# Row maxima spread over 64 rows by two DMAs, and a mask added on two tiles of three: an attention stage on one core

## The chip, the cores and the metric

The kernel runs on one core of one Trainium2 chip, in one launch. Its time is the device time of that core in microseconds; the time before is the median of three runs.

## The reference

A trunk of four residual layers on 1024 tokens of width 1024: attention, an MLP, a spatial gating layer, a second MLP, and a final norm. All of the change lies in the attention layer, which has 16 query heads of width 64 in two groups of eight:

```
# group A: band of 3 blocks of 128 keys, a sink logit for each head
s = einsum('bnqhgd,bnjhd->bnhgqj', qb, kband) * scale
s = where(mask, s, -1e30)                       # |key - query| <= 128
m = maximum(max(s, axis=-1), sink_b)
p = exp(s - m);  denom = sum(p) + exp(sink_b - m)
# group B: all 1024 keys
s = einsum('bqhd,bkhd->bhqk', qblk, kf) * scale
p = softmax(s)
```

Both groups need, for each query, the largest score m before the exponentials are taken.

## The kernel before

Everything runs as float32 split into a high part and a rest, so most products are made of several 128x512 matmuls. The attention layer first projects (tiles `lin`), writes rotated q and k to DRAM (`qs_...`), and then goes through the 16 heads in the order b b a a b a b a b a b a b a b a (`heads`, line 535); I call them h0 to h15. `load_head` (line 557) brings a head's q back by three DMAs: lines 568 and 569 fill both halves of `r1` with the high part, line 570 fills rows 0 to 63 of `r2` with the rest. Where a key group is new, `load_k` (line 547) first loads `k1` and `k2` by three more.

A head has two passes. The **maxima pass** (`mx_units`, line 574) multiplies 128 queries with the keys (`mx`, queries as rows of the result), and VectorE takes the maximum of each row: line 603 for a b head, line 587 for an a head. After four query tiles the four columns of maxima are put together in a 128x4 tile `m4` (lines 606 and 593); that is one set, two sets for each head. The **score pass** (`st_units`, line 698) makes the scores transposed (`st`, keys as rows), so that a maximum has to be subtracted from a column. It is therefore put into the product: rows 64 to 127 of `r2` hold -m/64 on every row, rows 64 to 127 of `k2` hold ones, and the sum over 64 rows gives -m. ScalarE takes the exponential, and `av` multiplies with the values.

What brings `m4` to these 64 rows is `bcast` (line 611): two steps of a chain after the set is done, four matmuls of 128 columns with a -1/64 identity turn and spread it in a PSUM bank (`bc`), and VectorE copies 64 rows of that into `r2` (line 617). For an a head the band's mask is a third matmul on each `st` tile, `identn` times `maskk`, 384 columns wide (256 at the two ends of the sequence).

The heads overlap: while head n is in its score pass, the maxima pass of heads n+1 and n+2 runs in between (`mx_to`, line 763). `load_to(n + 3)` (line 755) issues the loads. The program's order on each engine is set by a scheduler when the kernel is built, and every engine then works its list strictly in turn; so does SP, which issues all DMAs, and a DMA on SP that waits holds up those listed behind it. Eight PSUM banks are shared by all of these tiles.

Of the kernel before, what the change touches and what calls it, by code (L numbers as in the profile page):

```python
# [7 lines left out]
F32 = mybir.dt.float32  # L8
F32R = mybir.dt.float32r
AF = mybir.ActivationFunctionType  # L10
# [3 lines left out]
P = 128  # L14
# [3 lines left out]
HN = 512  # L18
# [14 lines left out]
def tile_kernel(ctx: ExitStack, tc: tile.TileContext, I, out, upto=99, dbg=None):  # L33
    nc = tc.nc
    pe, act, dve, pool, sp = nc.tensor, nc.scalar, nc.vector, nc.gpsimd, nc.sync
# [7 lines left out]
    drp = ctx.enter_context(tc.tile_pool(name="drp", bufs=1, space=bass.MemoryType.DRAM))  # L43
# [3 lines left out]
    def nm(s):  # L47
        uid[0] += 1
        return f"{s}_{uid[0]}"

    def blk(s, dt=F32R):
        return blkp.tile([P, 2, HN], dt, tag="blk", name=nm(s))

    def tr(s, dt=F32):
        return trp.tile([P, HN], dt, tag="tr", name=nm(s))
# [7 lines left out]
    def ps(s):  # L63
        return psp.tile([P, HN], F32, tag="ps", name=nm(s))

    def f(ap):
        return ap.bitcast(F32)
# [3 lines left out]
    def mm(o, l, r, start, stop, **kw):  # L71
        last_mm[0] = pe.matmul(o, l, r, start=start, stop=stop, **kw)  # L72
# [226 lines left out]
    def split(dst, src, lo=None):  # L299
        act.copy(dst[:, 0], src)  # L300
        (lo or dve).tensor_tensor(dst[:, 1], src, f(dst[:, 0]), op=ALU.subtract)
# [86 lines left out]
    with tc.issue_after(w_dma[5].ins):  # L388
# [3 lines left out]
        identn = cp.tile([P, P], F32R, name="identn")  # L392
# [115 lines left out]
    maskk = cp.tile([P, 3 * P], F32R, name="maskk")  # L508
# [30 lines left out]
    R1, R2 = {}, {}  # L539
# [3 lines left out]
    def kv_of(hd):  # L543
        return (0 if hd[0] == "a" else 2) + hd[1] // 4

    def load_k(kv):
        a = blk("k1")
        b = blk("k2")
        hi, lo = (qs["k"][part, kv].rearrange("r n t -> (r n) t") for part in range(2))
        sp.dma_start(f(a[0:64].rearrange("p a b -> p (a b)")), hi)  # L550
        sp.dma_start(f(a[64:128].rearrange("p a b -> p (a b)")), lo)
        sp.dma_start(f(b[0:64].rearrange("p a b -> p (a b)")), hi)
        pool.memset(f(b[64:128]), 1.0)
        k1[kv] = a.rearrange("p a b -> p (a b)")
        k2[kv] = b.rearrange("p a b -> p (a b)")

    def load_head(n):
        hd = heads[n]
        kv = kv_of(hd)
        if kv not in k1:  # L560
            load_k(kv)
        key = f"{hd[0]}{hd[1] // 4}"
        assert all((q, half) in ready for q in (key, "k") for half in range(2))
        hi, lo = (qs[key][part, hd[1] % 4].rearrange("r n t -> (r n) t") for part in range(2))
        a, b = blk("r1"), blk("r2")
        a = a.rearrange("p a b -> p (a b)")
        b = b.rearrange("p a b -> p (a b)")
        sp.dma_start(f(a[0:64]), hi)
        sp.dma_start(f(a[64:128]), hi)
        sp.dma_start(f(b[0:64]), lo)  # L570
        R1[n], R2[n] = a, b


    def mx_units(n):
# [34 lines left out]
        return [lambda tb=tb, kh=kh: unit(tb, kh) for tb in range(8) for kh in range(2)]  # L609

    def bcast(n, half, m4):
        for _ in range(2):
            yield 1
        p_ = ps("bc")
        for i in range(4):
            mm(p_[:, i * P : (i + 1) * P], m4[:, i : i + 1].to_broadcast([P, P]), identn, i == 0, i == 3)
        dve.tensor_copy(R2[n][64:128, half * HN : (half + 1) * HN], p_[64:128])
        shifted.add((n, half))

    OLO = pool  # L620
# [14 lines left out]
    def exps_b(p_):  # L635
        e = tr("pe")
        act.activation(e, p_, AF.Exp, scale=0.125)
        pp = blk("pp")
        cnt[0] += 1
        if cnt[0] % 4:  # L640
            act.copy(pp[:, 0], e)  # L641
        else:
            dve.tensor_copy(pp[:, 0], e)  # L643
        lo = dve if cnt[0] % 8 == 2 or (cnt[0] < 10 and cnt[0] % 2) else pool
        lo.tensor_tensor(pp[:, 1], e, f(pp[:, 0]), op=ALU.subtract)  # L645
        return pp
# [3 lines left out]
    def av(n, half, kt, pp, c0, o0, w_, first, last):  # L650

        kv = kv_of(heads[n])
        if (n, half) not in AV:
            AV[n, half] = ps("av")
        o = AV[n, half][:, o0 : o0 + w_]
        if kv < 2:
            mm(o, v1[kv][:, kt, :], pp[:, c0 : c0 + w_], first, last)
        else:
            a, b = v1[kv][:, kt, :], v2[kv][:, kt, :]
            mm(o, a, pp[:, 0, c0 : c0 + w_], first, False)  # L660
            mm(o, b, pp[:, 0, c0 : c0 + w_], False, False)
            mm(o, a, pp[:, 1, c0 : c0 + w_], False, last)
        if last:
            chains.append(finish_head(n, half))

    def finish_head(n, half):
        hd = heads[n]
        o = AV.pop((n, half))
        pair, r0 = (4 if hd[0] == "a" else 0) + hd[1] // 2, 64 * (hd[1] % 2)
        if pair not in O:  # L670
            O[pair] = blk("o", F32), blk("den", F32)
        yield 1
        rs = slice(r0, r0 + 64)
        out_, den = O[pair][0][:, half], O[pair][1][:, half]
        act.copy(out_[rs], o[0:64])
        if hd[0] == "a":
            es = tr("es")
            act.activation(es[64:128], f(R2[n][64:128, half * HN : (half + 1) * HN]), AF.Exp, scale=8.0,
                           bias=par[64:128, C_SINK + hd[1] : C_SINK + hd[1] + 1])
            dve.tensor_tensor(den[rs], o[64:128], es[64:128], op=ALU.add)  # L680
        else:
            act.copy(den[rs], o[64:128])
        if hd[1] % 2 == 0:
            return
        yield 1
        y = tr("rec")
        act.activation(y, den, AF.Ln)
        act.activation(y, y, AF.Exp, scale=-1.0)
        yield 1
        dve.tensor_tensor(den, den, y, op=ALU.mult)  # L690
        dve.scalar_tensor_tensor(y, den, 2.0, y, op0=ALU.subtract, op1=ALU.mult)  # L691
        dve.scalar_tensor_tensor(out_, out_, -1.0, y, op0=ALU.mult, op1=ALU.mult)
        yield 1
        t = blk("oh")
        split(t, out_, OLO)
        OH[pair, half] = t

    def st_units(n):
        hd = heads[n]

        def need(*halves):
            assert all((n, q) in shifted for q in halves), "row maxima come too late"

        kv = kv_of(hd)
        if hd[0] == "b":
            def unit(half, kt):
                need(half)
                p_ = ps("st")
                ks, hs = slice(kt * P, (kt + 1) * P), slice(half * HN, (half + 1) * HN)
                mm(p_, k1[kv][:, ks], R1[n][:, hs], True, False)  # L710
                mm(p_, k2[kv][:, ks], R2[n][:, hs], False, True)
                pp = exps_b(p_)
                return [lambda: av(n, half, kt, pp, 0, 0, HN, kt == 0, kt == 7)]

            return [lambda half=half, kt=kt: unit(half, kt) for half in range(2) for kt in range(8)]
        keep = {}

        plan = [(0, 0, True, False), (0, 3, False, False), (0, 1, False, False), (0, 2, False, False),
                (0, 4, False, True),
                (1, 4, True, False), (1, 7, False, False), (1, 5, False, False), (1, 6, False, False),  # L720
                (1, 3, False, True)]

        def score(kb):
            lo, hi = max(kb - 1, 0), min(kb + 2, 8)
            w_ = (hi - lo) * P
            off = (lo - kb + 1) * P
            need(lo // 4, (hi - 1) // 4)
            p_ = ps("st")[:, 0:w_]
            ks = slice(kb * P, (kb + 1) * P)
            mm(p_, k1[kv][:, ks], R1[n][:, lo * P : hi * P], True, False)  # L730
            mm(p_, identn, maskk[:, off : off + w_], False, False)
            mm(p_, k2[kv][:, ks], R2[n][:, lo * P : hi * P], False, True)
            keep[kb] = (exps_a(p_, w_), lo, hi)

        def part(half, kb, first, last):
            pp, lo, hi = keep[kb]
            a, b = max(lo, 4 * half), min(hi, 4 * half + 4)
            av(n, half, kb, pp, (a - lo) * P, (a - 4 * half) * P, (b - a) * P, first, last)

        def unit(items):  # L740
            for half, kb, first, last in items:
                if kb not in keep:
                    score(kb)
            return [lambda it=it: part(*it) for it in items]

        cuts = [plan[0:1], plan[1:2], plan[2:3], plan[3:4], plan[4:6], plan[6:7], plan[7:8], plan[8:10]]
        return [lambda c=c: unit(c) for c in cuts]
# [7 lines left out]
    def load_to(n):  # L755
        while loaded[0] < min(n, 16):
            load_head(loaded[0])
            loaded[0] += 1
# [603 lines left out]
```

## Time and profile before

| | before |
|---|---|
| median of 3 runs | 2074.59 us (2074.17 to 2076.68) |
| profiled execution, its own time | 2075.91 us |
| its span | 2074.1 us |
| busy, share of the span: TensorE / VectorE / ScalarE / GpSimd | 98% / 70% / 46% / 27% |
| attention's score pass | from about 164 to 451 us |

The span is what lies between the first and the last instruction. Matmuls overlap in their pipeline, so a matmul's own duration is longer than the step from its start to the next one's start, and a high busy share does not say that TensorE goes at full pace. Waits are given with the engine's instruction and with what ended the wait.

### The profile page before, as it was taken

The numbers are of one execution on the slowest core, as the hardware profiler recorded it, in microseconds if no ns is written. First come the engines' busy times: TensorE is split into PE (matmuls) and PEld (weight loads), VectorE is DVE, ScalarE is ACT, GpSimd is POOL, SyncE is SP. The second block draws the span as 40 slices with busy tenths as digits, with TensorE's granted clock in tenths as the row PEclk, the third lists the DMA queues.
The fourth block names the chain that finished last, engine by engine and source line by source line (L and its number), as shares of the span: only waits on it lengthen the run. The fifth ranks groups of instructions, "written<-read, shape, count | busy, mean of one in ns | idle before, by whom it ended". The sixth has DMA issues, their size and how long they took to land.

```text
span 2074.1 us, 27073 instructions
## 1 busy us (share of the span) xinstructions
PE 2028.4 (98%) x9126; PEld 1672.3 (81%) x9126; DVE 1456.5 (70%) x2324; ACT 962.2 (46%) x1768; POOL 563.8 (27%) x437
## 2 busy tenths in 40 slices
PE   8998999999999999999999999999999999999997
PEld 7786877788878888888888888888788888888885
DVE  6878878855896676756696445556976767846975
ACT  5525767763533333435444434533533333544542
POOL 4324565642232222200002125422232223000021
PEclk9999999999999999999999999999999999999998
DMA  4364121134135444767364210342254446865542
GB/s 163 128 185 135 40 68 36 42 112 152 52 132 171 149 157 163 266 206 289 128 220 142 92 59 11 122 138 97 76 180 150 148 162 205 296 222 191 170 139 92
DMA packets 207307, 294.92 MB, mean 142 GB/s; under 512 B 19648, under 2 KB 88768, under 8 KB 207168
## 3 DMA queue, kind: packets, MB, share of 16 engines
q1 hardware_dynamic: 207168, 293.19, 42.7%
q8 instruction: 72, 1.18, 0.2%
q14 instruction: 67, 0.55, 0.1%
HBM read 207.13 MB, written 85.98 MB: 141 GB/s over the span
## 4 chain that ended last, share of the span: by engine, by line
PE 85%; DVE 9%; issue 2%; ACT 2%; POOL 1%; DMA 1%; SPq 0%; DVEq 0%; POOLq 0%; ACTq 0%
PE up L72 26%; PE lin L72 17%; PE dy L72 17%; PE dx L72 13%; PE av L72 4%; PE st L72 3%; PE mx L72 1%; PE vp L72 1%; DVE w L147 1%; PE kp L72 1%; DVE mb L603 1%; DVE rec L691 1%; PE bc L72 1%; DVE pp L643 1%; PE hss L72 1%
## 5 line engine op out<-in xcount | busy, mean ns | idle before, releaser
L72 PE MATMUL up<-h,w 128*128 128x512 f32 x1536 | 363.1, 389 | 5.4 <-ACT w L146 3.0
L72 PE MATMUL dy<-w,w 128*128 128x512 f32 x1536 | 364.7, 389 | 0.0
L72 PEld LDWEIGHTS up<-h,w 128*128 128x128 f32 x1536 | 288.1, 188 | 66.1 <-ACT w L146 3.4
L72 PEld LDWEIGHTS dy<-w,w 128*128 128x128 f32 x1536 | 288.3, 188 | 60.3 <-issue 0.5
L314 POOL TENSOR_TENSOR ss<-ss,sq 128x512 f32<-128x512 f32 x66 | 103.1, 1563 | 661.7 <-ACT sq L313 566.8
L72 PE MATMUL dx<-w,w 128*128 128x512 f32 x1152 | 276.7, 389 | 0.0
L72 PE MATMUL up<-w,w 128*128 128x512 f32 x1152 | 276.6, 390 | 0.0
L72 PEld LDWEIGHTS up<-w,w 128*128 128x128 f32 x1152 | 216.2, 188 | 45.8 <-ACT h L835 0.5
L72 PEld LDWEIGHTS dx<-w,w 128*128 128x128 f32 x1152 | 216.2, 188 | 44.9
L146 ACT CAST w<-wr 128x512 fp32r<-128x512 f32 x288 | 167.5, 621 | 144.7 <-DVE wr L179 39.0
L147 DVE TENSOR_TENSOR w<-wr,w 128x512 fp32r<-128x512 f32 x288 | 201.6, 709 | 23.9 <-ACT w L146 19.9
L72 PE MATMUL lin<-h,w 128*128 128x512 f32 x768 | 181.3, 393 | 1.1 <-POOL w L123 0.5
L72 PEld LDWEIGHTS lin<-h,w 128*128 128x128 f32 x768 | 143.3, 188 | 33.6 <-issue 2.4
L956 POOL TENSOR_TENSOR t<-ua,ub 128x512 f32<-128x512 f32 x32 | 44.6, 1394 | 453.0 <-ACT ua L903 423.0
L645 POOL TENSOR_TENSOR pp<-pe,pp 128x512 fp32r<-128x512 f32 x107 | 143.0, 1358 | 77.7 <-ACT pp L641 54.2
L147 DVE TENSOR_TENSOR w<-ur,w 128x512 fp32r<-128x512 f32 x224 | 155.9, 706 | 6.6 <-ACT w L146 6.4
L146 ACT CAST w<-ur 128x512 fp32r<-128x512 f32 x224 | 135.9, 620 | 43.1 <-DVE w L147 20.5
L147 DVE TENSOR_TENSOR w<-ws,w 128x512 fp32r<-128x512 f32 x128 | 93.9, 734 | 68.6 <-ACT w L146 68.1
L72 PE MATMUL st<-r,k 128*128 128x512 f32 (+2 forms) x384 | 132.1, 402 | 4.6 <-DVE mb L603 3.6
L146 ACT CAST w<-ws 128x512 fp32r<-128x512 f32 x128 | 79.5, 621 | 112.0 <-DVE ws L226 75.8
L903 ACT ACTIVATE ua<-ua 128x512 f32<-128x512 f32 x64 | 40.5, 633 | 172.7 <-DVE ua L902 172.7
L72 PE MATMUL av<-pp,v 128*128 128x512 f32 x384 | 109.2, 395 | 3.5 <-DVE pp L643 1.6
(191 smaller groups left out, 3042.5 us busy)
## 6 DMA issues: line engine op xcount, KB each, us to landing
ur<-ucd SPq DMA_DIRECT2D x224, 256.0 KB, 3.6
wr<-in_w SPq DMA_DIRECT2D x256, 128.0 KB, 2.7
ucd<-t SPq DMA_DIRECT2D x128, 256.0 KB, 2.0
wr<-in_w SPq DMA_DIRECT2D x128, 256.0 KB, 3.7
ucd<-ub SPq DMA_DIRECT2D x64, 256.0 KB, 2.0
x<-in_xT SPq DMA_DIRECT2D x32, 256.0 KB, 3.5
xmd<-x SPq DMA_DIRECT2D x32, 256.0 KB, 2.1
ucd<-ua SPq DMA_DIRECT2D x32, 256.0 KB, 2.0
```

Of the source, the lines that this page charges most:

```text
L72: last_mm[0] = pe.matmul(o, l, r, start=start, stop=stop, **kw)
L146: act.copy(w[:, 0], src)
L147: dve.tensor_tensor(w[:, 1], src, f(w[:, 0]), op=ALU.subtract)
L314: pool.tensor_tensor(sumsq[half][:, 0:w_], sumsq[half][:, 0:w_], t, op=ALU.add)
L603: dve.tensor_reduce(M[n][:, tb, kh : kh + 1], p_, axis=AX.X, op=ALU.max)
L643: dve.tensor_copy(pp[:, 0], e)
L645: lo.tensor_tensor(pp[:, 1], e, f(pp[:, 0]), op=ALU.subtract)
L691: dve.scalar_tensor_tensor(y, den, 2.0, y, op0=ALU.subtract, op1=ALU.mult)
L903: act.activation(dst, dst, AF.Square)
L956: pool.tensor_tensor(t3, ua[:, 1], ub[:, 1], op=ALU.subtract)
```

## The change

Three edits. `bcast` now waits one step of its chain instead of two and issues two DMAs on SP: one writes the 128x4 set to a row of a DRAM tile `md`, element by element (512 runs of 4 bytes), the other reads that row of 2 KB into each of 64 rows of `r2`. The matmuls `bc` and the copy at line 617 go away. The scale -1/64 moves from `r2` to `k2`'s constant rows, and the sink's exponential takes a scale of -0.125 in place of 8. And the mask's matmul covers the two outer tiles of a band alone (2x128 columns in place of 384, 128 in place of 256).

```diff
-        pool.memset(f(b[64:128]), 1.0)
+        pool.memset(f(b[64:128]), -1.0 / 64.0)
...
+    md = drp.tile([16, 2, HN], F32, tag="md", name="md")
...
     def bcast(n, half, m4):
-        for _ in range(2):
-            yield 1
-        p_ = ps("bc")
-        for i in range(4):
-            mm(p_[:, i * P : (i + 1) * P], m4[:, i : i + 1].to_broadcast([P, P]), identn, i == 0, i == 3)
-        dve.tensor_copy(R2[n][64:128, half * HN : (half + 1) * HN], p_[64:128])
+        yield 1
+
+        row = md[n, half]
+        sp.dma_start(row.rearrange("(a q) -> q a", a=4), f(m4))
+        sp.dma_start(f(R2[n][64:128, half * HN : (half + 1) * HN]), row.partition_broadcast(64))
         shifted.add((n, half))
...
-            act.activation(es[64:128], f(R2[n][64:128, half * HN : (half + 1) * HN]), AF.Exp, scale=8.0,
+            act.activation(es[64:128], f(R2[n][64:128, half * HN : (half + 1) * HN]), AF.Exp, scale=-0.125,
...
-            mm(p_, identn, maskk[:, off : off + w_], False, False)
+            if 0 < kb < 7:
+                o_, m_ = (t.rearrange("p (a b) -> p a b", a=3)[:, ::2] for t in (p_, maskk))
+            elif kb:
+                o_, m_ = p_[:, 0:P], maskk[:, 0:P]
+            else:
+                o_, m_ = p_[:, P : 2 * P], maskk[:, 2 * P : 3 * P]
+            mm(o_, identn, m_, False, False)
```

On TensorE little else moves. Around the first set of h10, at the end of h8's score pass, before (tiles of the name `st` are scores, `av` values, `mx` maxima):

```order
L72 MATMUL st_823_3354<-r1_623_2705,k1_621_2699 128x512
L72 MATMUL st_823_3354<-r2_624_2706,k2_622_2700 128x512
L72 MATMUL av_822_3348<-pp_797_3268,v1_5_93 128x512
L72 MATMUL av_822_3348<-pp_797_3268,v2_6_95 128x512
L72 MATMUL av_822_3348<-pp_797_3268,v1_5_93 128x512
L72 MATMUL bc_826_3365<-identn_204,m4_815_3330 128x128 x4
L72 MATMUL st_829_3376<-r1_706_2966,k1_704_2960 128x256
L72 MATMUL st_829_3376<-maskk_766,identn_204 128x256
L72 MATMUL st_829_3376<-r2_707_2967,k2_705_2961 128x256
```

and the same place after:

```order
L72 MATMUL st_803_3277<-r1_609_2650,k1_607_2644 128x512
L72 MATMUL st_803_3277<-r2_610_2651,k2_608_2645 128x512
L72 MATMUL av_802_3269<-pp_777_3189,v1_5_93 128x512
L72 MATMUL av_802_3269<-pp_777_3189,v2_6_95 128x512
L72 MATMUL av_802_3269<-pp_777_3189,v1_5_93 128x512
L72 MATMUL st_808_3293<-r1_689_2899,k1_687_2893 128x256
L72 MATMUL st_808_3293<-maskk_766,identn_204 128x128
L72 MATMUL st_808_3293<-r2_690_2900,k2_688_2894 128x256
```

The four `bc` matmuls are gone and the mask is half as wide; nothing else changed its place.

On SP, before, the loads of h2 (`k1_334`, `k2_335`, `r1_336`, `r2_337`) follow straight behind the last writes of q:

```order
L461 DMA qs_a1_210<-qh_277_1577 128x2x512
L461 DMA qs_a1_210<-qh_278_1581 128x2x512
L550 DMA k1_334_1762<-qs_k_208 64x1024
L551 DMA k1_334_1762<-qs_k_208 64x1024
L552 DMA k2_335_1763<-qs_k_208 64x1024
L568 DMA r1_336_1768<-qs_a0_209 64x1024
L569 DMA r1_336_1768<-qs_a0_209 64x1024
L570 DMA r2_337_1769<-qs_a0_209 64x1024
```

After, both sets of h1 (`m4_284`, `m4_326`) stand in the same list ahead of them and between them:

```order
L461 DMA qs_a1_210<-qh_276_1574 128x2x512
L617 DMA md_1148<-m4_284_1597 128x4x1
L618 DMA r2_226_1349<-md_1148 64x512
L617 DMA md_1148<-m4_326_1732 128x4x1
L550 DMA k1_331_1753<-qs_k_208 64x1024
L618 DMA r2_226_1349<-md_1148 64x512
L551 DMA k1_331_1753<-qs_k_208 64x1024
L552 DMA k2_332_1754<-qs_k_208 64x1024
L568 DMA r1_333_1759<-qs_a0_209 64x1024
L569 DMA r1_333_1759<-qs_a0_209 64x1024
L570 DMA r2_334_1760<-qs_a0_209 64x1024
```

The first load now stands behind the write of `m4_326`, the others behind the read of it.

Later on SP, before, the loads of h11 (`r1_827`) and h12 (`r1_861`) stand alone:

```order
L568 DMA r1_827_3371<-qs_a1_210 64x1024
L569 DMA r1_827_3371<-qs_a1_210 64x1024
L570 DMA r2_828_3372<-qs_a1_210 64x1024
L568 DMA r1_861_3491<-qs_b1_212 64x1024
L569 DMA r1_861_3491<-qs_b1_212 64x1024
L570 DMA r2_862_3492<-qs_b1_212 64x1024
```

After, each stands behind a set of h10 (`m4_795` its first, `m4_823` its second, both into `r2_725`):

```order
L617 DMA md_1148<-m4_795_3251 128x4x1
L618 DMA r2_725_3025<-md_1148 64x512
L568 DMA r1_806_3288<-qs_a1_210 64x1024
L569 DMA r1_806_3288<-qs_a1_210 64x1024
L570 DMA r2_807_3289<-qs_a1_210 64x1024
L617 DMA md_1148<-m4_823_3354 128x4x1
L568 DMA r1_839_3404<-qs_b1_212 64x1024
L618 DMA r2_725_3025<-md_1148 64x512
L569 DMA r1_839_3404<-qs_b1_212 64x1024
L570 DMA r2_840_3405<-qs_b1_212 64x1024
```

The loads of a head have moved behind the write and the read of a set of the head before it.

## Rows read from the trace of the kernel before

**Rows 1.** Stretches (us): busy time and count by engine, clock, DMA share, GB/s.

```profile
164.00:451.00 287.00, 270.57 (x1271) 221.58 (x1272) 233.17 (x419) 210.98 (x390) 167.89 (x127) 0.99 0.25 64
```

**Rows 2.** TensorE's waits from 186 to 430 us: waiting instruction, releaser, sum, times, longest.

```profile
PE bc L72 <- DVE m L606: 4.1, 3, 1.4
PE st L72 <- DVE mb L603: 3.0, 4, 0.9
PE bc L72 <- DVE m L593: 2.4, 3, 1.1
```

**Rows 3.** Timeline, TensorE, 299 to 302 us: start, us, engine, line, operation, count.

```profile
299.27 0.56 PE L72 MATMUL bc<-identn,m 128*128 128x128 f32 x4
299.66 0.33 PE L72 MATMUL st<-r,k 128*128 128x256 f32 x1
299.83 0.28 PE L72 MATMUL st<-maskk,identn 128*128 128x256 f32 x1
299.95 0.28 PE L72 MATMUL st<-r,k 128*128 128x256 f32 x1
...
301.38 0.34 PE L72 MATMUL st<-maskk,identn 128*128 128x384 f32 x1
301.56 0.35 PE L72 MATMUL st<-r,k 128*128 128x384 f32 x1
```

**Rows 4.** Groups by form: VectorE's copy at line 617, busy us, mean ns, idle before.

```profile
L617 DVE CAST r<-bc 64x512 fp32r<-64x512 f32 x32 | 22.2, 695 | 3.9 <-PE bc L72 2.9
```

**Rows 5.** DMA page: queue (packets, MB, share), issues (KB, us to landing).

```profile
q1 hardware_dynamic: 207168, 293.19, 42.7%
...
wr<-in_w SPq DMA_DIRECT2D x256, 128.0 KB, 2.7
...
st<-in_w_sT SPq DMA_DIRECT2D x8, 64.0 KB, 2.4
...
par<-in_par SPq DMA_DIRECT2D x1, 34.0 KB, 1.8
```

**Rows 6.** The 16 DMAs of line 569, 130 to 460 us.

```profile
DMA to landing us min/median/max: 3.9/4.7/8.0
```

**Rows 7.** Timeline, 182 to 198 us: SP, VectorE and TensorE around h2.

```profile
182.88 0.60 SPq L569 DMA_DIRECT2D r<-qs_a  x1
...
191.90 0.16 DVE L606 TENSOR_REDUCE m<-mb 128x4 fp32r<-128x8 f32 x1
...
197.84 0.28 PE L72 MATMUL mx<-k,r 128*128 128x256 f32 x1
```

**Rows 8.** Timeline, 214 to 221 us: h3's first set, h4's first maxima.

```profile
214.79 1.13 DVE L593 CAST m<-ma 128x4 fp32r<-128x4 f32 x1
...
220.83 0.39 PE L72 MATMUL mx<-k,r 128*128 128x512 f32 x1
```

**Rows 9.** Timeline, 308 to 319 us: h8's second set, h10's first maxima.

```profile
308.81 0.16 DVE L606 TENSOR_REDUCE m<-mb 128x4 fp32r<-128x8 f32 x1
...
318.38 0.39 PE L72 MATMUL mx<-k,r 128*128 128x512 f32 x1
```

**Rows 10.** Timeline, 334 to 348 us: h10's first set, h11's first maxima.

```profile
334.94 0.50 PE L72 MATMUL mx<-k,r 128*128 128x512 f32 x1
...
338.42 0.16 DVE L606 TENSOR_REDUCE m<-mb 128x4 fp32r<-128x8 f32 x1
...
347.09 0.46 PE L72 MATMUL mx<-k,r 128*128 128x256 f32 x2
```

**Rows 11.** Timeline, 439 to 450 us: the last set, weights and exponentials behind it.

```profile
439.30 0.74 DVE L593 CAST m<-ma 128x4 fp32r<-128x4 f32 x1
...
444.81 1.13 ACT L121 CAST w<-st 128x512 fp32r<-128x512 f32 x2
445.84 0.76 ACT L632 ACTIVATE ea<-st 128x256 f32<-128x256 f32 x2
...
449.85 0.59 PE L72 MATMUL av<-ea,v 128*128 128x256 f32 x2
```

## The prediction

> **What bounds the kernel now.** I began with the stretches. The change lies in the score pass of the attention layer, 287 us in which TensorE is busy for 270.6 and VectorE for 233 [rows 1]. So what counts is TensorE's list: its steps, and where it stands still. The steps I read from the timeline as start to next start, since a matmul's own duration overlaps the next: the four narrow matmuls of a set take 0.39 us together, a mask of 384 columns takes 0.18 and one of 256 columns 0.12 [rows 3]. The waits of TensorE come next: from 186 to 430 us it stood 4.1 and 2.4 us before the narrow matmuls because VectorE had the set not ready, and 3.0 us before score tiles because a PSUM bank was not yet reduced, 9.5 us in all [rows 2]. Last I looked at what stands around each set in time, since the new DMAs stand in SP's list with the loads of later heads.
>
> **What goes.** There are 32 sets (16 heads, two each). The narrow matmuls: 32 x 0.39 = 12.5 us off TensorE's list [rows 3]. They have no cover, because TensorE is the engine that sets this stage. The masks: of the eight tiles of a head six go from 384 to 256 columns, 48 x 0.06 = 2.9 us, and two from 256 to 128, where a step of 0.39 / 4 = 0.10 us in place of 0.12 gives 16 x 0.02 = 0.3 us. No row shows a matmul that reads and writes two pieces of 128 columns. It may cost what one of 256 columns does, 0.12, or two of 128, 0.20, which would turn 2.9 into a loss of 1.0; I take the first, which is nearest in columns, so 3.1 us with rounding. The waits for a set before a narrow matmul, 6.5 us, go with the matmuls. The 3.0 us before score tiles I count as gone too: VectorE loses 32 copies of 0.695 us, 22.2 us of its 233 [rows 1, 4]. That is 12.5 + 3.1 + 9.5 = 25.1 us. The constants and the sink's scale change no instruction's size: nothing. The shorter chain (one step, not two) only issues the DMAs sooner.
>
> The Trainium skill (TensorE: Matmul & The Clock Gate, Back-to-back issue gap) gives about 81 ns for a matmul of 128 columns in a stream with its weight loads. The trace has 98 ns here, and the trace decides; by the page the narrow matmuls would be worth 10.4 us in place of 12.5, and the forecast would be 2 us later.
>
> **What comes.** Each set is now a write (512 runs of 4 bytes) and, on SP, a wait until it has landed, then the read of 2 KB into 64 rows. TensorE needs the read late: a set is used tens of microseconds after it is made, so the read itself is hidden. But SP works its list in turn, and the order now has the loads of the next heads behind the write and the read of a set. Today the load of h2's `r1` is out at 182.88, 15 us before its first matmul at 197.84 [rows 7]; behind a set that lead is gone. So for each head I compare the time from the set to the first maxima matmul of the loaded head with the chain: landing of the write (W), 0.6 us for each issue on SP that stands between [rows 7], and 4.7 us from the issue of the second `r1` load to its landing [rows 6].
>
> W is in no row. Below: 34 KB in 128 runs land in 1.8 us. Above: all packets of the queue took 42.7% of 16 x 2074 us for 207168, 68 ns each; 32 for an engine add 2.2 us to 1.8, so 4.0. In between: 64 KB in 128 runs of 512 bytes land in 2.4 us, 128 KB in 256 such runs in 2.7, 0.3 us for 128 runs more, which for 512 runs makes 3.3 [rows 5]. I take 3.0 us, between the middle of the bounds and that last figure.
>
> - h2: its set is ready at 192.06, the first maxima matmul comes at 197.84, 5.8 us later [rows 7]. Behind the landing stand the read, `k1`, `k2` and the first `r1`: 3.0 + 4 x 0.6 + 4.7 = 10.1. Late by 4.3 us.
> - h4: from 215.92 to 220.83, 4.9 us [rows 8]; one narrow group less (0.4), seven value matmuls that now stand ahead (0.24 each by the steps of [rows 3], 1.7): 6.2. The chain is 3.0 + 0.6 + 4.7 = 8.3. Late by 2.1.
> - h6, h10, h12, h14: from 308.97 to 318.38, 9.4 us [rows 9], less two narrow groups and five masks: 8.3. The chain is 8.3. Just in time.
> - h8: the same with three issues more (1.8). Late by 1.8.
> - h7, h11, h13, h15: from the last maxima matmul of the set at 334.94 to the use at 347.09 are 12.15 us; without the wait of 1.4 that ended there [rows 2], a narrow group and five masks, 10.05. VectorE had the set 3.64 us after the matmul [rows 10]; two copies fewer ahead of it make 2.25, so 7.8 are left. The chain is 3.0 + 2 x 0.6 + 4.7 = 8.9. Late by 1.1, four times: 4.4.
> - h9: the same with three key loads ahead. Late by 2.9.
> - After the last set stand two weight tiles. It is ready at 440.04; the write, the read and a load bring the first tile at 448.3. ScalarE wants it for a cast at 444.81 and, working in turn, holds the exponentials behind it, which today are done at 446.6 and needed at 449.85 [rows 11]. About 4.3 us later on ScalarE, with 0.7 us of TensorE's work gone, is 1.8 us late.
>
> The sum of what is late is 4.3 + 2.1 + 1.8 + 4.4 + 2.9 + 1.8 = 17.3 us. The net is 25.1 - 17.3 = 7.8 us: the profiled execution of 2075.9 us becomes 2068.1, and as the median stands 1.3 us under that execution, 2067 is my forecast.
>
> With W = 1.8 only 6.9 us are late: 2056. With W = 4.0 the four heads that are just in time join, 13 chains in all, 13 us more: 2080.
>
> **The rivals.** *A long write makes it slower.* The place is SP's wait for a write of 4-byte runs, and the price is 13 us for each microsecond of W beyond 3.0. The gain is used up at W = 3.6, and it is slower by over 0.2% from W = 3.9. For it: no row has runs under 272 bytes, and every set is such a write. Against it: 512 runs are few, 32 for each DMA engine. At W = 4.2 the time is 2082. The Trainium skill (DMA: Bandwidth & Descriptors, Specifications) says that runs below 512 bytes are read, modified and written by the DMA engine. By that rule, with the per-run share of the upper bound doubled, W would be an estimated 6.2 us and the time about 2108.
>
> *The loads have slack that I overlook*, so that nothing is late and the whole 25.1 us are gained: 2049.5. For it: today the loads run 15 us ahead [rows 7], and a late load may fall where TensorE would have waited for VectorE. Against it: the order has them behind the sets, word for word.
>
> *VectorE's waits come back.* TensorE no longer stops before the narrow matmuls, but a little later before a PSUM bank that VectorE has not reduced; only 15.6 us are gained, 17.3 lost: 2076, no change. For it: part of today's waits are of that kind already (3.0 us, [rows 2]). Against it: VectorE has 22 us less to do, and each late load gives it time.
>
> **Chances.** Forecast, W from 1.8 to 3.4: 0.45. Long write: 0.27. Waits come back: 0.17. Slack: 0.11. About 0.2%, 4.1 us, is what a measurement of this kernel can tell from no change, so faster means under 2070.4 and slower over 2078.7. Faster: 0.43 of the forecast and 0.11 of slack, 0.54. No change: 0.02, the 0.17, and 0.04 of the long write near its turning point, 0.23. Slower: 0.23. The range of 2052 to 2083 leaves out about 0.09 on each side. The forecast's own range is 2056 to 2072.
>
> **What would show it.** In the profile after, TensorE should have no wait for a set, and waits for `r` and `k` tiles loaded from DRAM in their place: the longest at h2's first maxima matmul, about 4 us, smaller ones at h4, h8 and the a heads. The write's time to landing is W itself. A mask's step should be 0.12 us. VectorE's busy time should be 22 us less. ScalarE should wait about 4 us at the weight cast after the last set. The prediction is wrong if TensorE waits for no load at all, if W is far from 3 us, or if TensorE's waits for VectorE stay near 9 us.

## The result, and the profile after

The change makes the kernel slower: a median of 2176.86 us (2169.16 to 2181.07, six runs) against 2075.69 us for the kernel before (six runs), a ratio of 1.0482 with a 95% interval of 1.0469 to 1.0495. That is 101 us more; 2067 was forecast. The profiled execution has a span of 2167.4 us, 93.3 more than before. Nearly all of that arises in the score pass: the first matmul of the output projection comes at 544.03 us in place of 451.05, 93.0 us later.

The stretch, from 164 us to near its end (the columns are those of [rows 1]):

```profile
164.00:542.00 378.00, 277.43 (x1136) 223.08 (x1137) 213.84 (x386) 208.88 (x389) 168.58 (x127) 0.86 0.27 60
```

TensorE is busy for 277 us, a little longer than before although its list is shorter, and that in 378 us in place of 287, at a mean granted clock of 0.86 in place of 0.99. So the stage now has gaps, and a lower clock. What ended the gaps, in TensorE's waits from 160 to 543 us (against [rows 2]):

```profile
PE mx L72 <- DMA r<-qs_a: 44.8, 6, 8.6
PE st L72 <- DMA r<-md: 33.6, 8, 9.9
PE mx L72 <- DMA r<-qs_b: 15.2, 5, 5.6
PE av L72 <- POOL pp L646: 5.3, 5, 1.5
PE mx L72 <- DVE mb L605: 1.6, 2, 1.1
PE mx L72 <- DVE ma L589: 0.8, 1, 0.8
```

They sum to 101.3 us; the same view of before, from 160 to 451 us, has 16.0. The waits for VectorE are nearly gone. In their place stand 60.0 us for loaded q tiles, as foreseen in kind, and 33.6 us for the set's own read, which was thought hidden.

The issues of DMAs (KB, median us from issue to landing; against [rows 5, 6]):

```profile
r<-qs_a SPq DMA_DIRECT2D x24, 256.0 KB, 6.6
r<-md SPq DMA_DIRECT2D x32, 128.0 KB, 4.2
md<-m SPq DMA_DIRECT2D x32, 2.0 KB, 9.6
```

A write of 2 KB takes 9.6 us to land, longer than a load of 256 KB. What SP does with that is plain around h2 (timeline of SP, then of TensorE; against [rows 7]):

```profile
180.58 0.36 SPq L617 DMA_DIRECT2D md<-m  x1
189.74 0.45 SPq L618 DMA_DIRECT2D r<-md  x1
190.36 0.46 SPq L617 DMA_DIRECT2D md<-m  x1
...
199.22 0.45 SPq L618 DMA_DIRECT2D r<-md  x1
...
201.62 0.60 SPq L569 DMA_DIRECT2D r<-qs_a  x1
...
208.36 0.55 PE L72 MATMUL mx<-k,r 128*128 128x256 f32 x1 [8.60 <-DMA r<-qs_a]
```

SP issues a write, stands 9 us, issues the read, then does the same for the next set. h2's second `r1` load is issued at 201.62; it was at 182.88 before. Its first maxima matmul waits 8.60 us. Over 150 to 560 us SP's waits say the same:

```profile
SPq L618 <- DMA md<-m: 248.2, 31, 11.6
```

The write's packets don't account for its length. Between the landing of other transfers and the read of 223.90 only the write issued at 215.55 is under way. The DMA view of 216 to 223.8 us, with the busy tenths of the 16 engines in 40 slices of 0.2 us:

```profile
DMA  0057000000000090000000000000000000000000
...
DMA packets 529, 0.01 MB, mean 1 GB/s; under 512 B 528, under 2 KB 528, under 8 KB 528
```

Its 512 packets are in slices 3 and 4, so they are through 1.2 us after the issue. Then the engines do nothing for it (the lone 9 is one packet of an instruction queue) for another 7 us until the write counts as landed.

The lower clock shows behind such a gap. TensorE at 412 us:

```profile
412.10 0.87 PE L72 MATMUL mx<-k,r 128*128 128x256 f32 x2 [7.30 <-DMA r<-qs_a]
...
413.62 0.52 PE L72 MATMUL st<-r,k 128*128 128x384 f32 x1
413.94 0.41 PE L72 MATMUL st<-maskk,identn 128*128 128x256 f32 x1
414.15 0.52 PE L72 MATMUL st<-r,k 128*128 128x384 f32 x1
```

After 7.30 us without work a product of 384 columns takes 0.32 us from start to start, against 0.18 in [rows 3]: the granted clock is 0.50 from 412 to 416 us and was 1.00 in the rows before, the 1.2 GHz level in place of 2.4. At 539 us, at the higher level (1.00 from 539.2 to 540 us), the mask's two pieces of 128 columns take a step of 0.13, about what one piece of 256 columns takes in [rows 3]:

```profile
539.23 0.28 PE L72 MATMUL st<-maskk,identn 128*128 128x256 f32 x1
539.36 0.33 PE L72 MATMUL st<-r,k 128*128 128x384 f32 x1
```

### The profile page after: what moved, and what is told of

Read it like the earlier page. It is cut to its first block, busy times and chain, and to the rows that moved or that the text cites. A ratio compares the mean times of both kernels' runs of the same rounds, so it can differ in the third digit from the quotient of the medians.

```text
span 2167.4 us, 26922 instructions
## 1 busy us (share of the span) xinstructions
PE 2036.6 (94%) x8998; PEld 1674.6 (77%) x8998; DVE 1437.9 (66%) x2292; ACT 961.2 (44%) x1768; POOL 564.9 (26%) x437
## 4 chain that ended last, share of the span: by engine, by line
PE 70%; DVE 6%; DMA 3%; issue 1%; ACT 1%; POOL 1%; SPq 0%; DVEq 0%; ACTq 0%; POOLq 0%
PE up L72 25%; PE dy L72 16%; PE lin L72 14%; PE dx L72 12%; DMA md<-m 2%; PE av L72 1%; DVE w L147 1%; PE st L72 1%; DMA r<-qs_a 1%; PE mx L72 0%; PE mix L72 0%; DVE mb L605 0%; DVE d L862 0%; PE ssb L72 0%; POOL vh L301 0%
## 5 line engine op out<-in xcount | busy, mean ns | idle before, releaser
L72 PE MATMUL st<-r,k 128*128 128x512 f32 (+2 forms) x384 | 144.6, 439 | 33.7 <-DMA r<-md 33.6
L72 PE MATMUL mx<-k,r 128*128 128x512 f32 (+2 forms) x192 | 73.9, 415 | 62.5 <-DMA r<-qs_a 44.8
L72 PEld LDWEIGHTS st<-r,k 128*128 128x128 f32 x384 | 80.4, 211 | 54.5 <-DMA r<-md 30.3
```

## The experiments

My theory after the result: the write of packed 4-byte runs is long, and by SP's list it makes loads and sets late. Rivals: the mask has a part; the number of runs, or their size, makes the write long whatever their place; the short runs hold the DMA engines, so that loads are late in any list; SP's standing still as such, not the chain's length, is what is paid.

**The mask alone** (kernel before, with the last block of the diff). 

> The kernel before with the mask's edit alone; the sets still go by four matmuls and a copy. My theory (everything lost comes from the sets' DMAs, the mask's edit is worth what the prediction said): 48 x 0.06 + 16 x 0.02 = 3 us faster, a ratio of 0.9985. Rival (a matmul in two pieces of 128 columns costs two matmuls of 128): 1 us slower, a ratio of 1.0005.

Measured: 2075.01 us against 2076.68, a ratio of 0.9993 (0.9984 to 1.0002). That can't be told from no change, nor, by its upper end of 3.3 us, from the 3 us expected. Two matmuls' price, 1.0005, is outside.

**The sets alone** (the change without that block). 

> The change with its sets by DMA alone; the mask stays three tiles wide. My theory: within 5 us of the whole change, some 104 us slower than before, since the matmuls that the mask saves lie in a stage that now waits for DMAs. Rival (the mask has a part in the loss): under 90 us slower.

Measured: 2178.01 us, ratio 1.0491 (1.0477 to 1.0505). The sets' DMAs alone make a loss that can't be told from the whole one.

**128 runs of 16 bytes.**

```diff
-        sp.dma_start(row.rearrange("(a q) -> q a", a=4), f(m4))
+        sp.dma_start(row.rearrange("(q a) -> q a", a=4), f(m4))
```

> The change, but each set is written in 128 runs of 16 bytes in place of 512 runs of 4 bytes, to the same 2 KB. The maxima thus land in another order and belong to other queries, and the exponentials take a scale of 0.01 so that they stay finite. My theory (the number of runs makes the write long, and the loads wait behind it on SP): the write lands in 2.5 to 4 us in place of 9.6, TensorE's waits for r tiles fall from 94 us to under 25, and the time is 2065 to 2090. Rival (a short run's writing or DRAM's answer is long whatever their number): 8 to 10 us to land, and the time stays at 2165 to 2180.

Measured: 2072.51 us, ratio 0.9980 (0.9971 to 0.9989). The write lands in 2.2 us; TensorE waits 8.2 us for r tiles (from 160 to 450 us):

```profile
PE av L72 <- POOL pp L646: 7.0, 8, 1.5
PE mx L72 <- DMA r<-qs_a: 4.2, 1, 4.2
...
PE st L72 <- DMA r<-md: 2.1, 1, 2.1
PE mx L72 <- DMA r<-qs_b: 1.9, 2, 1.1
```

So nearly all of the loss goes with the write's form. The one load that waits long is h2's, 4.2 us.

**256 runs of 8 bytes** (as above, with `"(a q b) -> q a b", a=2, b=2`). 

> As the kernel with 16-byte runs, with 256 runs of 8 bytes for a set (the maxima again belong to other queries, exponentials with a scale of 0.01). Theory (a price for each run: 128 runs 2.2 us, 512 runs 9.6 us, so 0.019 us a run): 4.7 us to landing, and by the prediction's 13 us for each microsecond beyond W = 2.2 some 30 us over the 2072.5 of 16-byte runs: 2100. Rival (it is the size of a run: below a bound every write is long): 8 us or more, and 2150 or more; or 2 to 3 us and 2075.

Measured: 2083.81 us, ratio 1.0037 (1.0023 to 1.0051); 3.8 us to landing. The landing is a little under the count's 4.7, and the time well under the 2100 that went with it. Count and place both remain possible.

**Both DMAs of a set issued by GpSimd** (`pool.dma_start` in place of `sp.dma_start` in `bcast`). 

> The change, but the write and the read of a set are issued by GpSimd in place of SP, so that no load stands behind them; the write is as long as in the change. My theory (what counts is SP's list): the waits for r tiles loaded from q go from 60 us to under 10; GpSimd stands 9 us on each read, 45 us of its rest subtractions come late, and the time is 2080 to 2120. Rival (the short runs keep the DMA engines themselves busy, and loads are late in whatever list they stand): 2150 or more, with the loads still at 6 to 7 us to landing. Second rival (the sets themselves come too late for the scores): the waits for the set's own tile stay above 30 us.

Measured: 2250.93 us, ratio 1.0840 (1.0826 to 1.0855). TensorE's waits from 150 to 640 us:

```profile
PE st L72 <- DMA r<-md: 76.2, 9, 17.1
PE av L72 <- POOL pp L646: 75.9, 18, 10.2
```

TensorE waits for no load any more. But in the same stretch GpSimd now stands 197 us before reads of sets (27 times), and both what it subtracts and the sets themselves are late, as the second rival had it. The time expected was far off: the standing did not go, it moved to an engine that has work to do. This run does not settle whether the loads were late through the list or through the engines, since TensorE was late for other reasons.

**The read three steps later.**

```diff
         sp.dma_start(row.rearrange("(a q) -> q a", a=4), f(m4))
+        for _ in range(3 if n > 1 else 0):
+            yield 1
         sp.dma_start(f(R2[n][64:128, half * HN : (half + 1) * HN]), row.partition_broadcast(64))
```

> The change, but from the third head on the read of a set is issued three steps of its chain after the write, so that in SP's order the loads of the next head stand ahead of the read nearly everywhere; the write is as long as in the change. My theory (SP's list, not the write itself, makes the loads late): TensorE's waits for r tiles loaded from q go from 60 us to under 25, with what is left where a load stands behind an earlier read; the time is 2095 to 2140. Rival (loads are late since the short runs hold the DMA engines): the loads keep 6 to 7 us to landing, their waits stay above 45, and the time is 2160 or more.

Measured: 2168.07 us, ratio 1.0441 (1.0427 to 1.0455), 0.4% under the change. My expectation failed. The b heads' loads moved ahead of a read and their waits fell from 15.2 to 6.3 us, but those of the a heads rose from 44.8 to 53.2, behind another read. And a load that is now issued in the middle of a write lands late: the median of `r<-qs_b` from 150 to 560 us is 11.7 us, 6.0 in the change.

**The loads issued by GpSimd, the sets left on SP** (`pool.dma_start` in `load_k` and `load_head`). 

> The change, with the loads of the heads' q and k issued by GpSimd in place of SP; the sets stay on SP as in the change. If the loads are late because they stand behind the sets in SP's list: TensorE's 60 us of waits for r tiles loaded from q go to under 15, the 34 us for the set's own tile stay or grow to 50, GpSimd's list is some 50 us longer in this stage, and the time is 2105 to 2140. If they are late because a write under way holds whatever the DMA engines are given: the waits stay above 40 us and the time is 2150 or more.

Measured: 2178.99 us, ratio 1.0494 (1.0476 to 1.0511). TensorE's waits from 150 to 570 us:

```profile
PE st L72 <- DMA r<-md: 75.7, 15, 10.9
PE mx L72 <- DMA r<-qs_a: 32.3, 5, 8.3
```

Neither theory fits. The waits for loads halve, so SP's list had a part; but the waits for the sets more than double (the write now lands in 10.4 us), and the sum is 108 us where the change has 93.6. What the loads no longer wait, TensorE waits for the sets.

**One write and one read for a head** (`m8` of 128x8 after the last tile, one `bcast` for both halves). 

> The change with one write of 1024 packed runs of 4 bytes and one read of 4 KB in 64 rows for a head, in place of two sets: 16 waits of SP in place of 32. Theory (the time is SP's standing, some 8 us for each write, and packed writes wait only within a block, so twice the blocks take no longer): 8 to 11 us to landing, SP stands 130 to 160 us on reads in place of 248, and the loss of 101 us falls to about half: 2110 to 2140. Rival (each run has its price): 17 to 20 us to landing, SP stands as long as in the change, and 2165 or more. Second rival (what counts is how late a set is, not SP's standing): a set that is finished with its head comes later still, TensorE's waits for it grow beyond 34 us, and 2165 or more.

Measured: 2183.21 us, ratio 1.0517 (1.0502 to 1.0533). The write of 1024 runs lands in 9.3 us, so each run does not have its price. SP stands 142.6 us before reads in place of 248.2, as expected, and nothing is gained (SP's waits from 150 to 570 us, then TensorE's):

```profile
SPq L618 <- DMA md<-m: 142.6, 16, 10.3
SPq L617 <- DVE m L608: 94.4, 8, 15.1
SPq L617 <- DVE m L595: 82.3, 7, 20.9
```

```profile
PE st L72 <- DMA r<-md: 77.0, 11, 8.3
PE av L72 <- POOL pp L647: 16.3, 14, 2.2
...
PE mx L72 <- DMA r<-qs_a: 4.0, 1, 4.0
```

The second rival's signs came: the waits for loads are nearly gone, and those for sets are 77 us. But SP's standing as a whole did not fall: before the writes it now stands 177 us for VectorE's maxima, against 54 in the change. So this run does not show that the standing costs nothing. My reading, which no run tests alone: in all of these variants the chain of a write of 9 us and a read is longer than the lead that the order gives a set or a load; only where TensorE meets it changes.

**Eight forms of the write, beside the kernel before** (an extra write and a read of one element behind each set). 

> The kernel before, with a second write of each set to DRAM in one of eight forms, four sets each, and behind it on SP a read of one element of what was written, whose issue shows when the write has landed; nothing uses what is read. Forms: 512 runs of 4 bytes packed in 2 KB (as in the change), the same 64 bytes apart, the same 512 bytes apart; 128 runs of 4 bytes packed in 512 bytes, the same 512 bytes apart; 128 runs of 16 bytes packed in 2 KB, the same 512 bytes apart; 256 runs of 8 bytes packed in 2 KB. Theory of the count (each run has its price): 512 runs take 8 to 10 us however far apart, 128 runs of 4 bytes 2 to 3 us, 256 runs 4 us. Theory of the place (writes into one block of DRAM wait for each other; a block of 512 bytes takes 128, 64 or 32 runs in the three packed forms, which landed in 9.6, 3.8 and 2.2 us): 512 runs 512 bytes apart land in 2 to 4 us, and 128 packed runs of 4 bytes in 8 to 10 us.

Measured: 2104.06 us (one run). SP's waits before the reads of one element, summed over up to four sets of a form (150 to 520 us):

```profile
SPq L581 <- DMA fd<-m: 33.7, 4, 9.5
SPq L590 <- DMA fd<-m: 30.5, 4, 8.6
...
SPq L602 <- DMA fd<-m: 13.8, 4, 3.9
...
SPq L587 <- DMA fd<-m: 4.5, 3, 1.7
...
SPq L596 <- DMA fd<-m: 3.3, 4, 1.1
```

Each line is one form, five of the eight. From the issue of the write to that of the read behind it, by SP's timeline, without the one pair in which two writes overlapped:

```
line  form                                     us, write to read       runs in 64 bytes
581   512 runs of 4 bytes, packed              8.3, 8.9, 9.0, 10.0     16
590   128 runs of 4 bytes, packed              7.1, 7.9, 8.2           16
602   256 runs of 8 bytes, packed              3.3, 3.9, 4.1, 4.3       8
596   128 runs of 16 bytes, packed             1.4 four times           4
584   512 runs of 4 bytes, 64 bytes apart      2.2, 2.2, 3.6, 6.1       1
587   512 runs of 4 bytes, 512 bytes apart     1.8, 1.9, 2.1, 2.3       1
593   128 runs of 4 bytes, 512 bytes apart     1.4, 1.4, 1.4, 2.5       1
599   128 runs of 16 bytes, 512 bytes apart    1.4, 3.0, 3.0            1
```

The place decides. A quarter of the packed 4-byte runs takes nearly as long as all of them; the same 512 runs 512 bytes apart take a fifth. (The 6.1 was issued among loads.) The time grows with the number of runs that share a small stretch of memory, and 64 bytes apart is nearly far enough (2.2 to 3.6 us, against 1.8 to 2.3 at 512 bytes). With the two columns, an estimate is some 0.5 us for each run in such a stretch (8 us for 16, 4 for 8), as if each waited for the one before; for 4 it would give 2 us, and 1.4 was measured, no more than for runs that lie apart. Why it is so is not shown, and in the packed forms a run's size and the number of runs in 64 bytes change together, so the forms show that the place decides, not the law. The Trainium skill (DMA: Bandwidth & Descriptors, Specifications) has every transfer below 512 bytes read, modified and written. It gives no price, and here the size alone does not make a write long: runs of 4 and of 16 bytes land quickly too when they lie apart (1.4 to 3.0 us at 512 bytes).

**The change with its 512 runs 64 bytes apart.**

```diff
-    md = drp.tile([16, 2, HN], F32, tag="md", name="md")
+    md = drp.tile([16, 2, HN * 16], F32, tag="md", name="md")
...
-        sp.dma_start(row.rearrange("(a q) -> q a", a=4), f(m4))
-        sp.dma_start(f(R2[n][64:128, half * HN : (half + 1) * HN]), row.partition_broadcast(64))
+        sp.dma_start(row.rearrange("(a q s) -> q a s", a=4, s=16)[:, :, 0], f(m4))
+        sp.dma_start(f(R2[n][64:128, half * HN : (half + 1) * HN]), row[0:HN].partition_broadcast(64))
```

> The change with the same 512 runs of 4 bytes for a set, but 64 bytes apart in DRAM (32 KB for a set, filled with zeros once beforehand); the read takes the first 2 KB of that as 64 rows of 2 KB, so the maxima aren't subtracted, and the exponentials take a scale of 0.01. Number and size of the runs, both DMAs of a set and SP's order are those of the change. Theory of the place (packed 4-byte writes wait for each other in DRAM): 2 to 3.6 us to landing and 2070 to 2085, like 128 packed runs of 16 bytes. Theory of the count or of the size of runs: 8 us or more and 2160 or more.

Measured: 2068.54 us, ratio 0.9965 (0.9953 to 0.9978), 2.0 us to landing. With the same runs, the same two DMAs and the same order on SP, the loss is gone (what else differs is a fill with zeros beforehand and the exponentials' scale). TensorE's waits from 160 to 570 us, those for DMAs first of all:

```profile
PE av L72 <- POOL pp L650: 8.9, 9, 1.5
PE mx L72 <- DMA r<-qs_a: 3.8, 1, 3.8
...
PE st L72 <- DMA r<-md: 1.3, 1, 1.3
...
PE mx L72 <- DMA r<-qs_b: 0.3, 1, 0.3
```

**No transport at all.** 

> The change without any transport of the sets: no write, no read, no narrow matmul, no copy; the 64 rows are filled by one more load of q's rest for a head (256 KB, 16 in all), and the exponentials take a scale of 0.01, so that the result is not the reference's. It shows the most that the edits could gain. The prediction's sum: 25.1 us, so 2050. Theory that waits come back (TensorE meets VectorE, GpSimd and ScalarE a little later): 12.5 + 3.1 us and at most 3 of the 9.5 us of waits, so 2057 to 2061.

Measured: 2062.42 us against 2076.15, ratio 0.9930 (0.9916 to 0.9943): by the medians 13.7 us is about the most that the edits could gain (the spans of the profiled executions, 2074.1 and 2058.5 us, differ by 15.6). TensorE's waits from 160 to 447 us:

```profile
PE av L72 <- POOL pp L643: 7.3, 9, 1.4
PE mx L72 <- DVE mb L605: 4.6, 5, 1.5
PE st L72 <- DVE mb L605: 2.0, 4, 1.1
PE av L72 <- DVE mb L605: 1.5, 1, 1.5
PE st L72 <- DVE w L428: 1.5, 2, 0.8
PE mx L72 <- ACT ea L630: 0.7, 1, 0.7
PE st L72 <- DVE den L678: 0.5, 2, 0.2
```

They sum to 18.1 us. The waits for sets are gone, and more than as much stands before other tiles.

**A set turned before it is written.** One matmul turns 128x4 into 4x128, and each run has 512 bytes; the kernel before otherwise, with the mask's edit.

```diff
+        mm(p_[0:4, 0:P], m4, identn, True, True)
+        t4 = t4p.tile([4, P], F32, tag="t4", name=nm("t4"))
+        dve.tensor_copy(t4, p_[0:4, 0:P])
+        sp.dma_start(row.rearrange("(a q) -> a q", a=4), t4)
+        sp.dma_start(f(R2[n][64:128, half * HN : (half + 1) * HN]), row.partition_broadcast(64))
```

> The kernel before with the mask's edit, and a set turned by one matmul of 4 rows x 128 columns, copied by VectorE as 4x128, written in 4 runs of 512 bytes and read into the 64 rows. Theory: the write lands in about 2 us, one narrow matmul and a short copy are left of four and a long one: TensorE's list is 9 + 3 us shorter, loads behind sets cost about 8 us as with 16-byte runs, and 3 to 6 us come from VectorE's waits for a set coming back: 2070 to 2076. Rival (the prediction's sum holds once W is 2): 2060 to 2066.

Measured: 2066.18 us, ratio 0.9952 (0.9940 to 0.9965), better than my theory had it. The loads were not late here: TensorE waits 0.7 us for them, and from a write of four runs to its read SP's timeline has 1.2 to 2.0 us (once 4.6). The waits for a set (4.1 and 2.0 us) are back, as the matmul is.

**The same, with the read two steps later.** 

> The same with the read of a set two steps of its chain after the write, so that loads don't stand behind it. Theory: the waits for loads (about 8 us) go and the time is 5 to 8 us under that of the read right behind the write: 2064 to 2070. Rival (what is gained at a load comes back as a wait for VectorE, GpSimd or ScalarE): within 2 us of the other.

Measured: 2064.59 us, ratio 0.9948 (0.9934 to 0.9961). Of the 5 to 8 us expected 1.6 came, within what can't be told from nothing: there was no wait for loads left to remove. This is the fastest version that computes everything, 11 us under the kernel before and 2 above the run without any transport.

## Why the prediction was wrong

**The step that failed is W, the write's time to landing.** It was taken as 3.0 us, with 1.8 and 4.0 as bounds; it is 9.6. The upper bound priced packets: a share of the queue's time for each run, spread over 16 engines, 2.2 us. For the packets that was enough, as all 512 were through 1.2 us after the issue. What was left out is the time behind them: 7 us in which the engines show no packet of the write, and which go when the same 512 runs lie apart. No row of before has several writes into one small stretch of memory, so its 68 ns a packet were no bound on this. The runs were counted when their addresses should have been looked at.

**The price of W came out near, in part by luck.** 13 us for each microsecond beyond 3.0 makes 6.6 x 13 = 86, and 2153 us; measured 2177. But the 17.3 + 86 = 103 us were to be lost at loads, and TensorE waits 60.0 us for loads; the rest of the loss stands at the sets and in slower matmuls, for which the working had no term. The runs give two points on the way: from 2.0 us (2068.5) to 3.8 (2083.8) 8.5 us for each, from 3.8 to 9.6 (2176.9) 16.0 for each. At short writes the working is near: interpolated between its 6.9 us late at 1.8 and 17.3 at 3.0 it has 8.6 us late at W = 2.0, and TensorE waits 5.4 us for DMAs there. h2's wait, forecast as 4.3 at W = 3.0 and so 3.3 at 2.0, is 3.8 at 2.0; at 9.6 the same working has 10.9 and the trace 8.60. Of the rivals, the long write is what happened, with a W beyond that rival's too: its 6.2 and 2108 us rested on the size of the runs, and the cause is their place.

**"The read itself is hidden" failed at this W.** 9.6 us to landing, 0.5 for the issue and 4.2 for the read make 14.3 us, and behind another set of the same head 9 more. The leads are not tens of microseconds: before, h2's first set was ready at 203.77 us and first used by a score matmul at 216.01, 12.2 us later. TensorE now waits 33.6 us for sets, where none was forecast. At W = 2.0 it is 1.3 us and at 2.2 it is 2.1, so for a W near 3 the statement would have been nearly right.

**What goes was 25.1 us; without any transport 13.7 went by the medians, 15.6 between the profiled executions.** The matmuls' 12.5 + 3.1 = 15.6 us are not too much: in that run TensorE is busy for 2011.1 us in place of 2028.4, 17.3 less, and its waits in the stage are 18.1 - 16.0 = 2.1 us more. The narrow ones were even priced too low. The 0.39 us of [rows 3] is the shortest that the 32 steps from a group of four to the next matmul take; they go up to 0.75 and make 17.2 us in all. One of the longer ones, also at a granted clock of 1.00:

```profile
242.92 0.85 PE L72 MATMUL bc<-identn,m 128*128 128x128 f32 x4
243.61 0.67 PE L72 MATMUL st<-r,k 128*128 128x512 f32 x2
```

The 9.5 us of waits were wrongly counted as gain: as much waiting and a little more stands before other tiles when the sets are left out. That is the rival of the returning waits, and in this step it was right, with GpSimd's 7.3 us besides VectorE's. At W = 2.0 my sum would have been 2058; the run with runs 64 bytes apart, 2068.5, is some 10 us over it.

**The sum of the loss.** In the profiled executions: 101.3 - 16.0 = 85.3 us of waits more, 15.6 us of matmuls less by the prediction's price, which leaves 93.0 - 69.7 = 23.3 us that are neither. The pages of the change and of the run with runs 64 bytes apart say where they are:

```profile
PE 2036.6 (94%) x8998; PEld 1674.6 (77%) x8998; DVE 1437.9 (66%) x2292; ACT 961.2 (44%) x1768; POOL 564.9 (26%) x437
PE 2012.1 (97%) x8998; PEld 1651.7 (80%) x8998; DVE 1435.7 (70%) x2292; ACT 959.1 (46%) x1768; POOL 566.2 (27%) x438
```

The same 8998 matmuls keep TensorE busy 24.5 us longer in the change, at a mean granted clock of 0.974 in place of 0.996. So what is left over is matmuls that take longer, as they do behind the gap at 412 us. Where the gaps are short the sum nearly closes without such a term: with the runs 64 bytes apart it gives 23.5 us of waits - 16.0 - 15.6 = -8.1, and the span is 9.1 us shorter (2065.0 and 2074.1). No run changed the clock alone, so that all of it is the clock is argued, not shown. The prediction had no term for it.

**The smaller steps.** The mask's step was forecast as 0.12 us and is 0.13. VectorE's busy time over the whole span fell from 1456.5 to 1437.9 us, 18.6 in place of 22. At the weight cast after the last set ScalarE waits 9.24 us where about 4 were forecast (its 4.3 should have been 3.5 by its own 448.3 and 444.81), again W:

```profile
536.12 1.32 ACT L121 CAST w<-st 128x512 fp32r<-128x512 f32 x2 [9.24 <-DMA st<-in_w_att_out]
```

And the loads' landing was taken over from before as 4.7 us; those of line 569 now have a median of 6.0 [rows 6].

What stays open: how loads that are issued while such a write is under way are held up (they land in 11.7 us in the run with later reads). The runs show that it happens, on two queues, not where.

## What to carry to other kernels

Before a small transfer goes to DRAM, look at the addresses that its runs touch: a transposing write of 4-byte elements into packed rows puts 16 runs into 64 bytes, and took 9 us where 512-byte runs mostly took 1.2 to 2; turn the data on chip first. A chain of dependent DMAs is paid by its length against the lead that the order gives it; here moving its parts to other lists, or halving their number at the price of later sets, only moved the wait. And waits of the bound engine for its feeders are no gain to be counted with the work that is removed: leave everything out once and see what the most is. Read a step's price from all of its places, since the one in a short window can be the cheapest.

## What the runs showed of the hardware that I had not expected

- 128 packed writes of 4 bytes (512 bytes in all) took 7.1 to 8.2 us to land, 512 of them 512 bytes apart 1.8 to 2.3, and 1024 packed ones 9.3.
- The DMA engines showed no packet for most of that time: the 512 packets were through 1.2 us after the issue.
- Loads issued among such writes landed in 10 to 11.7 us (median of `r<-qs_b`, with the reads of the sets later in SP's order, 11.7), also when the write stood in GpSimd's queue and the loads in SP's (three loads at 233 to 234 us, median 10.0).
